# Six of twelve gate projection pairs moved out of the recurrence into a phase of their own, with two thirds of their tokens computed by Strassen's seven products

## The chip, the cores and the metric

The kernel runs on one core of one Trainium2 chip. A core has five engines that run side by side, each through its own instruction stream in order: TensorE for matmuls (PE in the profile, with its weight loads as PEld), VectorE (DVE), ScalarE (ACT), GpSimd (POOL) and SyncE (SP), which here issues every DMA. The metric is the device time of one execution in microseconds (us). Before the change it is 2398.26 us, the median of three runs (2398.25 to 2399.79).

## The reference

One layer of a diffusion backbone is computed for 1024 sample tokens and 128 prompt tokens of width 1024, all in fp32. One wide projection of the modulated input feeds everything:

```python
qm, km, vm, om, gates, qa, ka, va, gm, ga = _split(h @ w_in, SPLITS)
hm, C, n, m = mlstm_bidir(...)                       # recurrence in both directions, 4 heads
hm = rms_norm(hm, ...) * jax.nn.sigmoid(om)
ha = block_attention(...)                            # 8 query heads on 2 key heads
merged = jax.nn.sigmoid(gm) * (hm @ w_bm) + jax.nn.sigmoid(ga) * (ha @ w_ba)
x = layer_norm(ALPHA * x + g1 * (merged @ w_out), ...)
x = layer_norm(ALPHA * x + g2 * (jnp.square(jax.nn.relu(h2 @ w_up)) @ w_down), ...)
```

The change is about `om`, `gm` and `ga`, three gates of 1024 columns each, which nothing needs before the merge that comes after attention.

## The kernel before

**Precision.** Every large fp32 product is made of three matmuls. `split` writes a rounded copy (`hi`, by ACT, line 72) and the remainder (`lo`, by DVE, line 73) of each operand, and `mm3` sums hi·hi, hi·lo and lo·hi in PSUM (lines 78 to 80). So a product over 1024 inputs is 8 blocks of 128 with 3 matmuls each: 24 matmuls.

**Tiling.** The 1152 tokens lie transposed in three blocks `hT[0..2]` of 384 tokens, hi and lo. A *pair* (`proj_pair`) is 256 output columns: it loads its weights (two loads of 512 KB into the two buffers `raw`), splits them, and computes for 3 blocks and 2 halves of 128 columns one tile `g` of 24 matmuls, which DVE copies out of PSUM (line 250) for a store to DRAM. PSUM holds two `g` tiles (`psg`), so the copy of a tile must be done before the tile after next can start. A pair is 144 matmuls of 384 columns. The twelve gate pairs are four each of `om`, `gm`, `ga`, stored in `gad`.

**Stages in order of time.** Start and modulation (to about 143 us); the recurrence `mlstm` over four heads (143 to 969 us); the attention's prologue and attention (to about 1310 us); the gate and output projections; the feed-forward part, whose second half is done by the same Strassen scheme for 768 tokens (`up_halves`, line 1408).

**The recurrence and its filler.** A head is a backward pass of 7 units, each a load of keys and values (`kvt`), a `kv_update` (6 matmuls into `kvp`) and a new state `st` stored to `bsd`; then 9 forward steps of 4 units: scores `sp`, decay `sT` with its split `sh`/`sl`, the output `op` of 18 matmuls, the normalised `hs` that is transposed a step later, and the state update. These are short matmuls with long chains over ACT and DVE between them. PE is kept busy by `filler`, a generator that hands out other matmuls in chunks of 6: key/value projections of the later heads, `q` pairs, the attention's `q`, `k`, `v`, the late half of the modulation (`mod_late`), and at the end all twelve gate pairs. After each unit `pull` takes `left / units` of it, where `left` is the filler's total in the program's own estimate (0.16 us per matmul of 384) less `RESERVE = 26.0`, and `units` is 176 at the start. What is left runs beside the attention's prologue, which loads and splits keys and values (`KH`, `KL`, `VH`, `VL`).

**What sets the order.** Each engine's instructions are put in order when the kernel is built, by a scheduler that works with estimated durations; pieces of code that are written one after the other come out interleaved. On the chip each engine then keeps that order. A tile of a pool that is opened where a closed pool lay waits for the tiles that it overlaps.

## Time and profile before

The profiled execution took 2397.98 us, of which the span from the first to the last instruction is 2396.2 us.

| stage (us from the span's start) | PE busy | DVE busy | DMA busy share |
|---|---|---|---|
| 190 to 340, recurrence, head 0 | 149.85 of 150 | 83.43 | 0.50 |
| 400 to 470, recurrence with attention's q | 66.43 of 70 | 50.44 | 0.48 |
| 640 to 780, recurrence, heads 2 and 3 | 140.00 of 140 | 75.03 | 0.53 |
| 969 to 1010, filler beside the prologue | 41.00 of 41 | 16.17 | 0.43 |
| 1350 to 1400, plain projections | 50.00 of 50 | 15.24 | 0.57 |

PE's busy time is modelled: matmuls overlap in its pipeline, and each row's duration (about 0.33 us for 384 columns) is longer than the distance to the next one. What a matmul costs in a dense stretch is the distance from start to start.

### The profile page before, as it was taken

Reading aid. Unit: us, or ns where it says so; the run is one execution under the profiler, and the core shown is the slowest. Engines: PE = TensorE matmul, PEld = TensorE weight load, DVE = VectorE, ACT = ScalarE, POOL = GpSimd, SP = SyncE. Lnnn points to the kernel's source line nnn. Section 1 sums busy time; section 2 is a strip of 40 time slices with the busy share of each in tenths; the row PEclk is TensorE's granted clock in tenths of the full one; section 3 lists DMA queues with packets and bytes.
Section 4 is the critical chain, followed back from the end, with each engine's and each line's share of the span. In section 5 each row is a group of like instructions: output and inputs, shape, how many; then the busy total and the mean of one; then the engine's idle time right before and its main releaser. Section 6 shows DMA issues by size and latency. Waiting matters only on the chain.

```text
span 2396.2 us, 36004 instructions
## 1 busy us (share of the span) xinstructions
PE 2348.3 (98%) x13294; PEld 2125.0 (89%) x13294; DVE 1494.3 (62%) x2738; ACT 999.6 (42%) x2133; POOL 372.0 (16%) x582
## 2 busy tenths in 40 slices
PE   7999999999999999999999999999999999999997
PEld 4888888788999999989999999889999989999996
DVE  5645645745755564388787345679444686666777
ACT  3323433524433243266666323225333443444444
POOL 1000110201101011144443000010000221111111
PEclk9999999999999999999999999999999999999999
DMA  7265447445654743320001755334443452222223
GB/s 273 90 207 159 128 134 216 138 126 163 196 157 139 216 148 99 118 68 17 17 17 40 228 184 180 121 115 150 140 132 124 152 173 69 64 71 71 71 79 115
DMA packets 229745, 305.71 MB, mean 128 GB/s; under 512 B 18105, under 2 KB 168753, under 8 KB 229569
## 3 DMA queue, kind: packets, MB, share of 16 engines
q1 hardware_dynamic: 229568, 303.41, 40.3%
q8 instruction: 105, 1.72, 0.3%
q14 instruction: 72, 0.58, 0.1%
HBM read 236.55 MB, written 66.79 MB: 127 GB/s over the span
## 4 chain that ended last, share of the span: by engine, by line
PE 87%; DVE 6%; DMA 3%; ACT 2%; issue 1%; POOL 1%; SPq 0%; DVEq 0%; ACTq 0%; POOLq 0%
PE g L78 14%; PE g L80 13%; PE g L79 13%; PE u L1408 4%; PE d L78 3%; PE d L79 3%; PE d L80 3%; PE pp L1408 3%; PE pz L1408 3%; PE t L883 2%; PE u L80 2%; PE u L78 2%; PE u L79 2%; PE pa L79 2%; PE pa L80 2%; PE pa L78 2%
## 5 line engine op out<-in xcount | busy, mean ns | idle before, releaser
L78 PE MATMUL g<-th,wh 128*128 128x384 f32 x1088 | 370.9, 341 | 0.0
L80 PE MATMUL g<-th,wl 128*128 128x384 f32 x1088 | 365.9, 336 | 0.0
L79 PE MATMUL g<-tl,wh 128*128 128x384 f32 x1088 | 364.1, 335 | 0.0
L72 ACT ACTIVATE wh<-raw 128x1024 fp32r<-128x1024 f32 x180 | 188.5, 1057 | 310.8 <-PE d L80 142.0
L73 DVE TENSOR_TENSOR wl<-raw,wh 128x1024 fp32r<-128x1024 f32 x180 | 223.9, 1251 | 127.1 <-ACT wh L72 125.7
L78 PE MATMUL g<-wh,th 128*128 128x512 f32 x600 | 240.6, 401 | 1.4 <-ACT xq L654 0.8
L80 PE MATMUL g<-wh,tl 128*128 128x512 f32 x600 | 236.0, 393 | 0.0
L79 PE MATMUL g<-wl,th 128*128 128x512 f32 x600 | 235.4, 393 | 0.0
L78 PEld LDWEIGHTS g<-th,wh 128*128 128x128 f32 x1088 | 204.4, 188 | 8.6 <-issue 5.9
L80 PEld LDWEIGHTS g<-th,wl 128*128 128x128 f32 x1088 | 204.2, 188 | 0.4 <-issue 0.4
L79 PEld LDWEIGHTS g<-tl,wh 128*128 128x128 f32 x1088 | 204.5, 188 | 0.1
L1199 DVE TENSOR_TENSOR acc<-acc,d 128x512 f32<-128x512 f32 x160 | 109.4, 685 | 58.6 <-PE d L80 56.7
L78 PEld LDWEIGHTS g<-wh,th 128*128 128x128 f32 x600 | 112.8, 188 | 26.7 <-issue 3.8
L80 PEld LDWEIGHTS g<-wh,tl 128*128 128x128 f32 x600 | 112.7, 188 | 23.3
L79 PEld LDWEIGHTS g<-wl,th 128*128 128x128 f32 x600 | 112.9, 188 | 20.7 <-DVE wl L73 1.0
L72 ACT ACTIVATE ph<-t 128x384 fp32r<-128x384 f32 x192 | 91.0, 493 | 70.5 <-PE t L883 70.1
L250 DVE COPY fm<-g 128x384 f32<-128x384 f32 x96 | 53.2, 554 | 98.3 <-PE g L80 96.1
L73 DVE TENSOR_TENSOR pl<-t,ph 128x384 fp32r<-128x384 f32 x192 | 104.7, 548 | 9.0 <-ACT ph L72 7.2
L883 PE MATMUL t<-ident,pe 128*128 128x128 f32 x576 | 96.2, 276 | 6.2 <-DVE pl L73 5.1
L1312 POOL TENSOR_TENSOR wtl<-raw 128x512 f32<-128x512 f32 x16 | 20.7, 1295 | 486.3 <-PE pa L79 252.8
L872 POOL TENSOR_SCALAR pe<-pe,rs 128x1152 f32<-128x1152 f32 x64 | 79.0, 1235 | 55.0 <-DVE rs L871 27.6
L78 PE MATMUL pv<-ph,vh 128*128 128x256 f32 x288 | 85.6, 297 | 1.5 <-DVE tl L73 1.5
(398 smaller groups left out, 5899.9 us busy)
## 6 DMA issues: line engine op xcount, KB each, us to landing
raw<-in_w_up_dram SPq DMA_DIRECT2D x64, 512.0 KB
raw<-in_w_down_dram SPq DMA_DIRECT2D x64, 512.0 KB
raw<-in_w_in_dram SPq DMA_DIRECT2D x44, 512.0 KB
kvt<-kvd SPq DMA_DIRECT2D x64, 257.0 KB
raw<-in_w_mod_dram SPq DMA_DIRECT2D x32, 512.0 KB
kvd<-kvs SPq DMA_DIRECT2D x36, 257.0 KB
uw<-ud SPq DMA_DIRECT2D x72, 128.0 KB
bs<-st SPq DMA_DIRECT2D x32, 258.0 KB
```

The costliest lines, as they stand in the source:

```text
L72: nc.scalar.activation(out=hi, in_=src, func=AF.Copy)
L73: nc.vector.tensor_tensor(out=lo, in0=src, in1=f(hi), op=ALU.subtract)
L78: nc.tensor.matmul(out, lhsT=ah, rhs=bh, start=start and i == 0, stop=False)
L79: nc.tensor.matmul(out, lhsT=ah, rhs=bl, start=False, stop=False)
L80: nc.tensor.matmul(out, lhsT=al, rhs=bh, start=False, stop=stop and i == n - 1)
L250: nc.vector.tensor_copy(out=st[:], in_=g[:, 0:TB])
L872: nc.gpsimd.tensor_scalar(pe[:], pe[:], rs[:, 0:1], 1.0, ALU.mult, ALU.mult)
L883: nc.tensor.transpose(pt[:, k, :], pexp[u][:, kt * 128:kt * 128 + 128], ident[:])
L1199: nc.vector.tensor_tensor(out=y[:, cs], in0=y[:, cs], in1=g[:], op=ALU.add)
L1312: nc.gpsimd.tensor_tensor(out=tmp[i], in0=x, in1=y, op=op)
L1408: nc.tensor.matmul(o, lhsT=x[:, k, :], rhs=y[:, k, :], start=fresh and k == 0 and i == 0, stop=k == 3 and i == 2, skip_group_check=True)
```

## The change

Of the twelve gate pairs five (all `om`, first of `gm`) stay in the recurrence's filler (`NPL = 5`), and the reserve falls from 26 to 12. The filler of the recurrence so has 8 pairs instead of 15. `mod_late` may start a second time within a long job. The last pair (`ga` 3) stays plain and becomes the filler beside the attention's prologue.

The six pairs between them run in a new phase after the recurrence. Their first 384 tokens are computed as before (`plainS`, 48 matmuls, copied out by ACT). The 768 tokens of blocks 1 and 2 are taken as the two halves of a 2x2 block product (columns of the pair, inputs, tokens each halved) by Strassen's scheme in Winograd's form: seven products of 12 matmuls each (line 878 of the changed kernel) instead of eight, 84 matmuls instead of 96. For it

- the four token forms are made once by `t_formsS`: 16 additions (line 796) and 16 subtractions (line 802) on DVE, and 16 splits (ACT and DVE), spread by `building` over the rest of the recurrence's filler;
- per pair, POOL makes four weight combinations (`combS`, line 828 of the changed kernel, 128x512 each), ACT and DVE split them into a ring of three (`ufS`), ACT copies three sums and one result out of PSUM, and DVE makes five sums (line 866);
- new pools `psS` (four PSUM banks) and `sp` take the recurrence's place, and the attention's pools take theirs.

```diff
+    gpairs = [(a + 256 * p, gad[nm][p]) for nm, a in (("om", OM), ("gm", GM), ("ga", GA)) for p in range(4)]
+    NPL, RES = 5, 12.0
...
-        for nm, a in (("om", OM), ("gm", GM), ("ga", GA)):
-            jobs += [(proj_pair(a + 256 * p, gad[nm][p]), 24) for p in range(4)]
+        jobs += [(proj_pair(a, dst), 24) for a, dst in gpairs[:NPL]]
...
-                if c == 8 and mods:
+                if (c == 8 or c == 20 and n == 36) and mods and md is None:
                     md = mods.pop(0)
...
-    left = [6 * FT + 15 * FP - RESERVE]
+    left = [6 * FT + (3 + NPL) * FP - RES]
...
     st1.close()
+    psS = pool(sts_, "psS", 2, space=PSUM)
+    sp_ = pool(sts_, "sp", 1)
+    tS = {nm: tuple(sp_.tile([128, 4, TB], F32R, name="tS" + nm + e) for e in "hl") for nm in ("s1", "s2", "s3", "a22")}
...
+    def t_formsS():
+        src = {"a11": tS["a11"], "b12": tuple(t[:, 0:4, :] for t in hT[2]), "a12": tS["a12"], "s4": tS["s4"]}
+        for k in range(4):
+            full = []
+            for nm, t in src.items():
+                d = sft("f" + nm)
+                nc.vector.tensor_tensor(out=d[:], in0=f(t[0][:, k, :]), in1=f(t[1][:, k, :]), op=ALU.add)
+                full.append(d)
+                yield
+            b11, b12, b21, b22 = full
+            t3 = sft("ft3")
+            for dst, x, y, nm in ((t3, b22, b12, "s3"), (b11, b12, b11, "s1"), (b22, b22, b11, "s2"), (b21, b21, b22, "a22")):
+                nc.vector.tensor_tensor(out=dst[:], in0=x[:], in1=y[:], op=ALU.subtract)
+                split(tS[nm][0][:, k, :], tS[nm][1][:, k, :], dst[:])
+                yield
...
+    def halvesS(slots, c, w, dst, each):
...
+        for j, nm in enumerate(("a11", "a22", "a12", "s2", "s1", "s3", "s4")):
+            b = "xyxpzpz"[j]
+            fresh = b not in bank
...
+            for k in range(4):
+                for i, (x, y) in enumerate(((wh, bh), (wh, bl), (wl, bh))):
+                    nc.tensor.matmul(o, lhsT=x[:, k, :], rhs=y[:, k, :], start=fresh and k == 0 and i == 0,
+                                     stop=k == 3 and i == 2, skip_group_check=True)
...
+    building(fill)
+    preps.append(prepS(spairs[1][0]))
+    for i in range(2):
+        building(plainS(preps[i][1], spairs[i][1]))
+    run(build)
+    for i in range(n):
...
+        halvesS(preps[i][1], comb, fw_, spairs[i][1], each)
+        if "fill" in nxt:
+            fill = nxt["fill"]
+            next(fill)
+        if i + 1 < n:
+            comb, fw_ = nxt["c"], nxt["w"]
+            if i:
+                run(plainS(preps[i + 1][1], spairs[i + 1][1]))
```

How this comes out in the engines' order is shown at three places.

**The filler in the last head, on SP.** Each forward step of the recurrence ends in one store `hmd<-ho`; each `<-fm` is the store of one filler tile of 24 matmuls. Before:

```order
L69 DMA hmd_4_177<-ho 128x256
L66 DMA kvt<-kvd_8_133 128x514
L69 DMA ga_1_245<-fm 128x384
L69 DMA ga_2_246<-fm 128x384
L66 DMA raw<-in_w_in_dram 128x4x256
L69 DMA ga_2_246<-fm 128x384
L66 DMA raw<-in_w_in_dram 128x4x256
L69 DMA hmd_5_178<-ho 128x256
L69 DMA ga_0_247<-fm 128x384 x2
L69 DMA ga_1_248<-fm 128x384
L69 DMA hmd_6_179<-ho 128x256
```

The same place now:

```order
L69 DMA hmd_4_177<-ho 128x256
L66 DMA kvt<-kvd_8_133 128x514
L69 DMA om_1_227<-fm 128x384
L69 DMA om_2_228<-fm 128x384
L69 DMA hmd_5_178<-ho 128x256
L66 DMA raw<-in_w_in_dram 128x4x256
L69 DMA om_2_228<-fm 128x384
L66 DMA raw<-in_w_in_dram 128x4x256
L69 DMA om_0_229<-fm 128x384
L69 DMA hmd_6_179<-ho 128x256
```

Between two step stores there stood three tiles, now two. On PE, in this head, the scores `sp` of a step and its `op` were 36 filler matmuls apart in the usual step, now 24.

**DVE at the end of the recurrence.** `no<-pt` is the recurrence's last small output. Before, what followed were copies of filler tiles (`fm<-g`) and the split of the attention's keys (`kl`):

```order
L646 COPY no<-pt 16x128
L250 COPY fm<-g 128x384 x2
L73 TENSOR_TENSOR kl<-pe,kh 128x512 x2
L250 COPY fm<-g 128x384
L73 TENSOR_TENSOR kl<-pe,kh 128x512 x2
L250 COPY fm<-g 128x384
```

Now the token forms (`Sf...`, `tS...`) stand there. This is the stretch from the second to the third copy, which is repeated twice more:

```order
L250 COPY fm<-g 128x384
L73 TENSOR_TENSOR tSs3l<-Sft_9584,tSs3h 128x384
L73 TENSOR_TENSOR tSs1l<-Sfa_9560,tSs1h 128x384
L802 TENSOR_TENSOR Sfs_9576<-Sfs_9576,Sfa_9560 128x384
L796 TENSOR_TENSOR Sfb_9611<-th,tl 128x384
L802 TENSOR_TENSOR Sfa_9574<-Sfa_9574,Sfs_9576 128x384
L73 TENSOR_TENSOR tSs2l<-Sfs_9576,tSs2h 128x384
L796 TENSOR_TENSOR Sfa_9609<-th,tl 128x384
L73 TENSOR_TENSOR tSa22l<-Sfa_9574,tSa22h 128x384
L796 TENSOR_TENSOR Sfs_9625<-th,tl 128x384
L796 TENSOR_TENSOR Sfa_9623<-th,tl 128x384
L802 TENSOR_TENSOR Sft_9633<-Sfs_9625,Sfb_9611 128x384
```

One more (line 802) follows before the next copy, so 12 DVE instructions stand between one tile's copy and the next, where there were none to two.

**PE in the same stretch.** `g` is a filler tile of the recurrence's last pair, `Sx` the first Strassen product:

```order
L80 MATMUL g<-th,wl 128x384
L878 MATMUL Sx<-th,wh 128x384
L878 MATMUL Sx<-tl,wh 128x384
L878 MATMUL Sx<-th,wl 128x384
L878 MATMUL Sx<-th,wh 128x384
L878 MATMUL Sx<-tl,wh 128x384
L878 MATMUL Sx<-th,wl 128x384
L878 MATMUL Sx<-th,wh 128x384
L878 MATMUL Sx<-tl,wh 128x384
L878 MATMUL Sx<-th,wl 128x384
L878 MATMUL Sx<-th,wh 128x384
L78 MATMUL g<-th,wh 128x384
```

The scheduler has put 10 to 12 matmuls of the first two products between filler tiles, four tiles before the filler ends. From the recurrence's last instruction on PE to the first tile of `plainS` there are 7 whole filler tiles and the rest of one, where 11 whole ones stood before attention's first transposes; beside the attention's prologue there are now 6.

More of the change, by code (lines that the diff above doesn't have):

```diff
@@ L772, in hybrid_step_kernel, with sft @@
     st1.close()
+    sts_ = ctx.enter_context(ExitStack())
+    psS = pool(sts_, "psS", 2, space=PSUM)
+    sp_ = pool(sts_, "sp", 1)
+    tS = {nm: tuple(sp_.tile([128, 4, TB], F32R, name="tS" + nm + e) for e in "hl") for nm in ("s1", "s2", "s3", "a22")}
+    tS["a11"] = tuple(t[:, 0:4, :] for t in hT[1])
+    tS["a12"] = tuple(t[:, 4:8, :] for t in hT[1])
+    tS["s4"] = tuple(t[:, 4:8, :] for t in hT[2])
+    ufS = sp_.tile([128, 6, 512], F32R, name="ufS")
+    cntS = [0]
+    def sft(nm, w=TB):
+        return sp_.tile([128, w], F32, tag=nm, name="S" + nm)
@@ new lines, in hybrid_step_kernel, with prepS @@
+    wiv = kview(w_in)
+    def prepS(a):
+        raws, slots = [], []
+        for q in range(2):
+            raw = rp.tile([128, 1024], F32, tag="raw", name="raw")
+            rv = raw[:].rearrange("p (k n) -> p k n", n=256)
+            load(rv, wiv[:, 4 * q:4 * q + 4, a:a + 256])
+            hi = wp.tile([128, 1024], F32R, tag="wh", name="wh")
+            lo = wp.tile([128, 1024], F32R, tag="wl", name="wl")
+            split(hi[:], lo[:], raw[:])
+            raws.append(rv)
+            slots.append(tuple(t[:].rearrange("p (k n) -> p k n", n=256) for t in (hi, lo)))
+        return raws, slots
@@ new lines, in combS @@
+    def combS(raws):
+        a11, a21 = raws[0][:, :, 0:128], raws[0][:, :, 128:256]
+        a12, a22 = raws[1][:, :, 0:128], raws[1][:, :, 128:256]
+        c = {}
+        for nm, x, y, op in (("s1", a21, a22, ALU.add), ("s2", "s1", a11, ALU.subtract), ("s3", a11, a21, ALU.subtract),
+                             ("s4", a12, "s2", ALU.subtract)):
+            t = sft("c" + nm, 512)[:].rearrange("p (k n) -> p k n", n=128)
+            nc.gpsimd.tensor_tensor(out=t, in0=c[x] if isinstance(x, str) else x, in1=c[y] if isinstance(y, str) else y, op=op)
+            c[nm] = t
+        return c
@@ new lines, in plainS, with formS @@
+    def plainS(slots, dst):
+        for m in range(2):
+            g = gtile()
+            w = [tuple(t[:, k % 4, 128 * m:128 * m + 128] for t in slots[k // 4]) for k in range(KT)]
+            yield from mm3g(g[:, 0:TB], [(w[k], (hT[0][0][:, k, :], hT[0][1][:, k, :])) for k in range(KT)], 2, C384)
+            st = fmp.tile([128, TB], F32, tag="fm", name="fm")
+            nc.scalar.activation(out=st[:], in_=g[:, 0:TB], func=AF.Copy)
+            store(dst[0][:, m, :], st[:])
+    def formS(src):
+        j = cntS[0] % 3
+        cntS[0] += 1
+        hi, lo = (ufS[:, j + 3 * e, :].rearrange("p (k n) -> p k n", n=128) for e in range(2))
+        split(hi, lo, src)
+        return hi, lo
@@ new lines, in hybrid_step_kernel, with building, each @@
+    spairs = gpairs[NPL:11]
+    n = len(spairs)
+    preps = [prepS(spairs[0][0])]
+    comb = combS(preps[0][0])
+    fw_ = begin_forms(comb)
+    build = t_formsS()
+    def building(gen):
+        for _ in gen:
+            next(build, None)
+            next(build, None)
+    building(fill)
[4 more added lines that the diff above has]
+    for i in range(n):
+        nxt = {}
+        def each(j):
+            if j == 3:
+                if i + 1 < n:
+                    nxt["c"] = combS(preps[i + 1][0])
+            elif j == 5 and i + 2 < n:
+                preps.append(prepS(spairs[i + 2][0]))
+            elif j == 5 and i + 2 == n:
+                nxt["fill"] = proj_pair(*gpairs[11])
+            elif j == 6 and i + 1 < n:
+                nxt["w"] = begin_forms(nxt["c"])
+        halvesS(preps[i][1], comb, fw_, spairs[i][1], each)
+        if "fill" in nxt:
+            fill = nxt["fill"]
+            next(fill)
+        if i + 1 < n:
+            comb, fw_ = nxt["c"], nxt["w"]
+            if i:
+                run(plainS(preps[i + 1][1], spairs[i + 1][1]))
@@ L775, in hybrid_step_kernel @@
+    sts_.close()
     st2 = ctx.enter_context(ExitStack())
```

38 lines of the change are left out of this document (added).

## The prediction

> **What bounds the kernel now.** First the page: the busy line and the chain of work that ended last.
>
> ```profile
> span 2396.2 us, 36004 instructions
> ...
> PE 2348.3 (98%) x13294; PEld 2125.0 (89%) x13294; DVE 1494.3 (62%) x2738; ACT 999.6 (42%) x2133; POOL 372.0 (16%) x582
> ...
> PE 87%; DVE 6%; DMA 3%; ACT 2%; issue 1%; POOL 1%; SPq 0%; DVEq 0%; ACTq 0%; POOLq 0%
> ```
>
> TensorE is busy 98% of the span and holds 87% of the last chain. Busy time alone can hide slow matmuls, so the next view is by stages; columns are the stretch, its length, then busy time of PE, PEld, DVE, ACT and POOL with counts, PE clock, DMA share, GB/s.
>
> ```profile
> 143.00:190.00 47.00, 46.46 (x241) 37.08 (x240) 24.96 (x60) 12.82 (x32) 3.42 (x19) 1.00 0.71 214
> 190.00:340.00 150.00, 149.85 (x828) 125.01 (x827) 83.43 (x190) 61.78 (x171) 21.43 (x53) 1.00 0.50 148
> 340.00:400.00 60.00, 60.00 (x342) 54.21 (x341) 32.58 (x72) 19.96 (x49) 4.06 (x15) 1.00 0.65 200
> 400.00:470.00 70.00, 66.43 (x355) 53.56 (x354) 50.44 (x99) 39.00 (x123) 16.84 (x29) 1.00 0.48 144
> 540.00:640.00 100.00, 99.36 (x571) 86.60 (x570) 66.46 (x141) 48.38 (x153) 19.72 (x33) 1.00 0.56 171
> 780.00:836.00 56.00, 56.00 (x351) 52.97 (x350) 29.39 (x67) 15.96 (x38) 3.64 (x9) 1.00 0.73 224
> 836.00:969.00 133.00, 132.24 (x844) 128.51 (x843) 72.87 (x158) 51.77 (x119) 16.70 (x26) 1.00 0.40 122
> 1010.00:1060.00 50.00, 47.30 (x320) 43.58 (x318) 34.54 (x77) 28.69 (x76) 20.67 (x28) 1.00 0.23 73
> ```
>
> The clock is full throughout. In these stretches of the recurrence PE idles 0.54 + 0.15 + 3.57 + 0.64 + 0.76 = 5.7 us, most of it in 400 to 470, where the attention's q is prepared beside it. So the kernel is bound by the number of matmuls, and whatever the filler covers is really covered.
>
> **The term that gains: 12 matmuls less per pair.** What a plain matmul costs is read from start to start in a stretch that has nothing else (timeline, the first and the last of 217 starts, nine tiles of 24 between), what a Strassen product costs from one run of seven products in the feed-forward part (stages, line 1408 alone).
>
> ```profile
> 1360.12 0.33 PE L78 MATMUL g<-th,wh 128*128 128x384 f32 x1
> ...
> 1397.56 0.33 PE L78 MATMUL g<-th,wh 128*128 128x384 f32 x1
> ...
> 1928.20:1942.93 14.73, 14.72 (x84) 14.54 (x83) 1.00 0.60 190
> ```
>
> Plain: 37.44 / 216 = 0.1733 us. The two later blocks of a pair are 96 of them, 16.64 us. The 84 of the seven products take 14.72 us, 0.1752 each. Six pairs gain 6 x 1.92 = **11.5 us**. The 48 matmuls per pair on the first block, the seven other pairs, the recurrence itself and all weight loads stay in number.
>
> **The token forms: DVE against the filler's copies.** PE's filler tiles need their PSUM bank copied by DVE, and 12 form instructions stand between two copies. Durations and spacing are those of the same work in the feed-forward part (timeline), the copy's and the split's from the page.
>
> ```profile
> 1656.23 0.55 DVE L1131 TENSOR_TENSOR va<-th,tl 128x384 f32<-128x384 f32 x1
> 1656.69 0.55 DVE L1131 TENSOR_TENSOR vs<-th,tl 128x384 f32<-128x384 f32 x1
> ...
> L73 DVE TENSOR_TENSOR wl<-raw,wh 128x1024 fp32r<-128x1024 f32 x180 | 223.9, 1251 | 127.1 <-ACT wh L72 125.7
> L250 DVE COPY fm<-g 128x384 f32<-128x384 f32 x96 | 53.2, 554 | 98.3 <-PE g L80 96.1
> ```
>
> One starts 0.47 us after the other, though each lasts 0.55. So 13 instructions from copy to copy take 6.1 us. PE has in that time a tile, 24 x 0.1733 = 4.16 us, and 10 to 12 Strassen matmuls, 1.8 to 2.1 us: 5.9 to 6.3 us. The two are even. Ahead of it DVE has two weight splits, three weight forms and six token instructions, about 7.5 us, while PE has two free banks, 8.3 us. I charge 0.2 us for each of the three stretches and 0.6 us for POOL's combinations, which run in the middle: **1.2 us**. From both sides: nothing, or, if each instruction took its whole 0.55 us, 48 x 0.08 = 3.9 us more.
>
> POOL slows DVE where both read; the feed-forward part shows how much (groups, 1920 to 2200 us, the same split beside POOL and away from it; below them POOL's own combination on the page).
>
> ```profile
> L73 DVE TENSOR_TENSOR uf<-wtl,uf 128x512 fp32r<-128x512 f32 x18 | 21.1, 1174 | 11.2 <-ACT uf L72 11.2
> ...
> L73 DVE TENSOR_TENSOR uf<-wth,uf 128x512 fp32r<-128x512 f32 x18 | 12.4, 689 | 12.9 <-ACT uf L72 12.8
> ...
> L1312 POOL TENSOR_TENSOR wtl<-raw 128x512 f32<-128x512 f32 x16 | 20.7, 1295 | 486.3 <-PE pa L79 252.8
> ```
>
> The split that meets POOL takes 0.49 us longer. Three combinations, those of the second pair, fall among the forms: 1.5 us of DVE, of which 0.6 us reaches PE through a bank. The Trainium skill, "SBUF — State Buffer", "Who interferes with whom", says that a DVE instruction with two SBUF inputs and a POOL instruction that reads SBUF exclude each other for the whole instruction. By that rule DVE would lose up to 3 x 1.3 = 3.9 us there; this trace shows less than half of it per meeting.
>
> **The recurrence with less cover.** By the program's numbers the filler per unit falls from 596 / 176 = 3.39 us to 449 / 176 = 2.55 us. What hangs on it is the slack of each chain (timeline, last head: scores, decay, its split, the product; the earlier step's normalised output and its transpose; then a backward unit).
>
> ```profile
> 877.24 0.35 DVE L621 TENSOR_SCALAR hs<-hs,ss 128x256 f32<-128x256 f32 x1 [0.77 <-POOL ss L620]
> 879.93 0.61 PE L578 MATMUL sp<-qt,kT 128*128 128x128 f32 x4
> 881.56 0.55 DVE L73 TENSOR_TENSOR sl<-sT,sh 128x256 fp32r<-128x256 f32 x1 [0.55 <-ACT sh L72]
> 883.50 0.38 PE L562 MATMUL pt<-ident,hs 128*128 128x128 f32 x2
> 887.13 0.28 PE L78 MATMUL op<-vh,sh 128*128 128x258 f32 x1
> ...
> 801.11 0.42 DVE L73 TENSOR_TENSOR wkl<-wk,wkh 128x256 fp32r<-128x256 f32 x1
> 803.58 0.28 PE L78 MATMUL kvp<-vh,wkh 128*128 128x258 f32 x1
> ```
>
> `sl` ends at 882.11, 5.0 us before its product; with 12 matmuls less (2.1 us) 2.9 us stay. `hs` ends 5.9 us before its transpose; 18 matmuls less in that place, 3.1 us, leave 2.8. `wkl` has 2.05 us, and its unit loses about 1. So the usual step still waits for nothing. The waits that are there already grow: cover falls by a quarter, and I let the 5.7 us of idle time grow by half, **2.8 us**, the bounds being 0 and 12 us (0.07 us in each of 176 units).
>
> **Attention starts with less cover.** The keys' loads and splits follow the phase's last stores on SP, and 6 tiles (25 us) beside them are ample, since the prologue waits only for its DMAs. But the first units no longer have three tiles behind their scores. Their chain is these (groups of attention, then the page):
>
> ```profile
> L865 DVE TENSOR_REDUCE nm<-sa 128x1 f32<-128x768 f32 x52 | 49.5, 951 | 5.4 <-PE sa L80 5.4
> ...
> L868 ACT ACTIVATE pe<-sa,nm 128x768 f32<-128x768 f32 x52 | 46.5, 895 | 0.0
> L867 ACT ACTIVATE pe<-sb,nm 128x384 f32<-128x384 f32 x52 | 30.2, 581 | 26.3 <-DVE nm L866 21.6 <-PE t L883 2.9 <-DVE tl L73 0.4
> ...
> L872 POOL TENSOR_SCALAR pe<-pe,rs 128x1152 f32<-128x1152 f32 x64 | 79.0, 1235 | 55.0 <-DVE rs L871 27.6
> ```
>
> 0.95 + 0.58 + 0.90 + 1.24 and some 1.2 us of small steps are 4.9 us, against 18 matmuls, 3.1 us, of the next two units: **1.5 us**, bounds 0 and 4.9.
>
> **Inside the phase** a pair takes 14.7 + 8.3 = 23 us on PE and some 8 us each on DVE and ACT, and POOL 4 x 1.3 us; the loads are two per pair as before, but wait for POOL to be done with `raw`. The place without plain tiles, between the first two pairs, is the tightest. **0.4 us**, bounds 0 and 3.
>
> **Sum.** -11.5 + 1.2 + 2.8 + 1.5 + 0.4 = -5.6 us against the profiled execution's 2397.98 us (0.3 us under the median of the runs): **2392.4 us**. 0.2%, 4.8 us, is about what a measurement of this kernel can tell from no change.
>
> **Rivals.**
> *The cover's loss takes most of the gain.* If the idle time of 400 to 470, where DVE is busy 72% already, and that of the later q stretch (540 to 640) double, 4.2 us, and each head's backward pass loses 0.5 us more, the recurrence costs 6.2 us instead of 2.8: 2395.8 us, no change. For it: 3.57 of 5.7 us idle time lie there. Against: the slacks above.
> *POOL and DVE exclude each other.* Each of three combinations stops DVE for its whole 1.3 us, 3.9 us that reach PE through the banks in full: 3.3 us over what I charge, 2395.7 us, no change. For it: DVE and PE are even there, so no slack takes it up. Against: 0.49 us per meeting. This is the rule of the Trainium skill named above; by it this rival holds.
> *The recurrence becomes bound by DMA; slower.* Its bytes stay, but its time shrinks by about a quarter. From the stages: 143 to 190 holds 0.71 x 47 = 33 us of full DMA and will have about 34; 780 to 836 holds 41 and will have 43; 340 to 400 holds 39 for 46. As long as the queues can be kept over nine tenths full, nothing is lost. If only 0.8 can be used, the three need 42, 51 and 49 us, 19 us more if all of it reached PE; I count 11, since loads that run ahead take some of it up: 2403.4 us. It makes the kernel slower from a usable share of about 0.8 downwards. Against it stand two short stretches in which DMA ran full while PE was never idle:
>
> ```profile
> 135.00:140.00 5.00, 5.00 (x26) 3.55 (x25) 1.25 (x6) 0.00 (x0) 0.00 (x0) 1.00 0.96 284
> 160.00:165.00 5.00, 4.99 (x26) 3.91 (x24) 1.67 (x4) 1.42 (x4) 0.57 (x1) 1.00 1.01 264
> ```
>
> *The change doesn't do what it says.* If a product waited for its accumulating bank (ACT must copy `Sx` before the third product adds to it), 0.15 us in each of the 42 products would be 6.3 us and the gain gone: 2398.7 us. The feed-forward part does the same at 0.1752 us per matmul, so hardly.
>
> **How the numbers follow.** My forecast has 0.46; the cover's loss 0.27, the exclusion 0.07, no gain in the products 0.04, together 0.38 for no change; DMA 0.16 for slower. The range reaches down to 2385.5, the whole gain at no cost and 1 us of today's idle time gone with it, and up to 2402.5: costs of 16 us, two thirds of the sum of their upper bounds (5.1 + 12 + 4.9 + 3), which takes in part of the DMA case.
>
> **What would show it.** In the changed profile: 84 matmuls of line 878 in 14.7 us; PE idle under 2 us between the last `hs` transpose and the first tile of `plainS`; under 9 us of idle time in the recurrence, which should end near 812 us (969 less 147 us of filler by the program's numbers, each of 0.16 us being 0.1733); DMA shares under 0.95 in its backward passes; attention's first transposes within 2 us of the scores of its third unit. Waits of PE for `wkl` or `sl`, or single gaps over 2 us among the forms, would make the prediction wrong.

## The result, and the profile after

The changed kernel takes **2420.71 us** (median of four runs, 2418.94 to 2422.81) beside 2399.03 us for the kernel before on the same chip: ratio 1.0087, 95% interval 1.0075 to 1.0100. It is 21.7 us slower; 2392.4 was forecast, and the range ended at 2402.5. The profiled execution took 2418.94 us, 20.96 more than the one of before.

The page first: span, busy line, and shares of the chain that ended last.

```profile
span 2417.1 us, 36076 instructions
...
PE 2346.6 (97%) x13222; PEld 2115.2 (88%) x13222; DVE 1534.5 (63%) x2804; ACT 1037.3 (43%) x2209; POOL 408.1 (17%) x606
...
PE 55%; DVE 4%; ACT 2%; issue 1%; DMA 1%; POOL 1%; DVEq 0%; ACTq 0%; POOLq 0%
```

The 72 matmuls are gone (13294 to 13222), and PE is still busy 97%. Where the time went is read by stages. The view by stretches of the changed kernel: first the recurrence from its first `kvp` to its last `hs` transpose, then the first part of the phase, its rest, and attention. Columns as in the prediction: stretch, length, busy PE, PEld, DVE, ACT, POOL, then clock, DMA share, GB/s.

```profile
145.00:830.00 685.00, 664.92 (x3900) 571.31 (x3900) 428.82 (x968) 306.16 (x839) 105.50 (x234) 1.00 0.57 171
830.00:872.00 42.00, 37.34 (x205) 36.59 (x204) 36.91 (x60) 13.09 (x24) 14.89 (x7) 0.96 0.20 61
872.00:1021.00 149.00, 146.62 (x845) 145.98 (x844) 50.77 (x70) 43.42 (x72) 29.46 (x23) 1.00 0.33 103
1021.00:1332.00 311.00, 300.83 (x2132) 278.00 (x2132) 243.63 (x572) 202.47 (x516) 129.25 (x193) 1.00 0.10 30
```

The same stretches of the kernel before (recurrence, then the prologue's filler, then attention):

```profile
143.00:969.00 826.00, 820.33 (x4823) 730.97 (x4821) 468.73 (x1021) 323.62 (x854) 108.11 (x234) 1.00 0.53 159
969.00:1001.00 32.00, 32.00 (x187) 31.84 (x186) 11.73 (x18) 6.49 (x11) 4.15 (x6) 1.00 0.50 155
1001.00:1310.00 309.00, 299.86 (x2141) 279.99 (x2140) 239.74 (x567) 198.70 (x511) 129.69 (x192) 1.00 0.09 27
```

Length less busy PE is PE's idle time: the recurrence went from 5.67 to **20.08 us**, the phase from 0.00 to 4.66 + 2.38 = 7.04, attention from 9.14 to 10.17. That is 22.5 us more, but -11.5 + 22.5 is only half of the 21 us by which the profiled execution is longer. The rest is in the busy column: a row is longer than the distance to the next one, so a matmul that starts a little late leaves no idle time. A second measure catches it: the distance from each matmul's start to the next, less the usual step of its shape (0.1733 us for 384 columns, 0.227 for 512, 0.104 to 0.120 for the short ones), summed and called *lost time* below. It went from 39.8 to 58.9 us in the recurrence, 0.1 to 8.9 in the phase, 27.0 to 30.7 in attention and 33.2 to 34.0 elsewhere: 32.4 us more. With 72 matmuls fewer (12.5 us by the same steps) that makes 19.9, and 20.96 was measured; the short matmuls' steps are rough, so a sum of this kind holds to about 1 us.

Who is waited for in the recurrence, changed kernel (columns: in all us, times, longest):

```profile
PE pt L550 <- ACT ho L565: 3.9, 4, 1.3
PE g L79 <- DVE wl L73: 3.7, 4, 1.5
PE pt L562 <- ACT qs L685: 2.3, 2, 1.4
PE g L78 <- ACT xq L654: 1.9, 1, 1.9
PE kvp L78 <- ACT wkh L72: 1.4, 3, 1.0
```

The same list of the kernel before begins so:

```profile
PE pt L550 <- ACT ho L565: 1.6, 3, 0.8
PE pt L683 <- ACT kT L552: 1.6, 1, 1.6
PE g L78 <- ACT xq L654: 0.8, 1, 0.8
```

No single wait took over. Many grew, and ACT stands behind most: `ho`, `qs` and `kT` are its copies out of the one PSUM bank `t`, which all transposes share, and `xq` its copy out of a `g` bank.

The idle time can be split in two ways. The first is by the recurrence's own passes. The four backward passes idle 0.5 us before and 7.9 us after, the forward passes 5.1 and 12.2 us. So half of the rise lies in the backward passes, which are a fifth of the recurrence's time. The last one, in the kernel before and after:

```profile
792.50:828.60 36.10, 36.10 (x227) 34.27 (x226) 19.47 (x45) 8.64 (x20) 0.79 (x2) 1.00 0.72 221
```

```profile
682.80:719.40 36.60, 33.98 (x208) 30.30 (x208) 25.45 (x53) 15.55 (x41) 5.71 (x6) 1.00 0.80 243
```

The DMA share of these passes is 0.80 to 0.89 after the change (0.58 to 0.86 before). After the change PE waits there mostly for the unit's own chain (`wkh`, `wkl`, `st`) and for the weights' splits (`wl`).

The second split is by the filler's jobs, whose stretches take in the backward passes. There the lost time lies in the six token jobs (keys/values, attention's k/v and q): 21.8 us before, 44.1 after (some 8 us of the rise are only the matmuls of six more modulation halves that now run in them, about 1.4 us each, for which the steps above have no price; in the pair jobs they are missing). One of them, attention's second `q` job, in the kernel before and after:

```profile
558.50:623.30 64.80, 64.16 (x343) 53.13 (x342) 43.73 (x95) 34.48 (x119) 15.06 (x26) 1.00 0.52 154
```

```profile
609.10:687.60 78.50, 73.20 (x405) 57.53 (x404) 52.75 (x113) 43.74 (x144) 20.18 (x34) 1.00 0.46 139
```

The stretch of the same job now has 405 matmuls, the job's own among them, instead of 343, since more units of the recurrence and a second modulation half fall on it, and with them 144 instead of 119 ACT instructions. Its idle time goes from 0.64 to 5.30 us.

### The profile page after: what moved, and what is told of

The parts are those of the page before. It is cut to its first block, busy times and chain, and to the rows that moved or that the text cites. A ratio compares the mean times of both kernels' runs of the same rounds, so it can differ in the third digit from the quotient of the medians.

```text
span 2417.1 us, 36076 instructions
## 1 busy us (share of the span) xinstructions
PE 2346.6 (97%) x13222; PEld 2115.2 (88%) x13222; DVE 1534.5 (63%) x2804; ACT 1037.3 (43%) x2209; POOL 408.1 (17%) x606
## 4 chain that ended last, share of the span: by engine, by line
PE 55%; DVE 4%; ACT 2%; issue 1%; DMA 1%; POOL 1%; DVEq 0%; ACTq 0%; POOLq 0%
PE g L79 5%; PE g L78 5%; PE g L80 5%; PE u L1575 4%; PE d L78 3%; PE d L80 3%; PE d L79 3%; PE pp L1575 3%; PE pz L1575 2%; PE t L1050 2%; PE u L80 2%; PE u L78 2%; PE u L79 2%; PE pa L79 2%; PE pa L80 2%; PE pa L78 2%
## 5 line engine op out<-in xcount | busy, mean ns | idle before, releaser
L78 PE MATMUL g<-th,wh 128*128 128x384 f32 x896 | 304.9, 340 | 4.7 <-DVE fm L250 4.7
L80 PE MATMUL g<-th,wl 128*128 128x384 f32 x896 | 301.6, 337 | 0.0
L79 PE MATMUL g<-tl,wh 128*128 128x384 f32 x896 | 300.2, 335 | 0.0
L78 PEld LDWEIGHTS g<-th,wh 128*128 128x128 f32 x896 | 168.8, 188 | 9.9 <-DVE fm L250 5.5
L79 PEld LDWEIGHTS g<-tl,wh 128*128 128x128 f32 x896 | 169.0, 189 | 0.0
L80 PEld LDWEIGHTS g<-th,wl 128*128 128x128 f32 x896 | 168.6, 188 | 0.0
L78 PE MATMUL u<-th,wh 128*128 128x384 f32 x256 | 85.7, 335 | 0.0
```

The lines of the kernel that those rows point to most:

```text
L78: nc.tensor.matmul(out, lhsT=ah, rhs=bh, start=start and i == 0, stop=False)
L79: nc.tensor.matmul(out, lhsT=ah, rhs=bl, start=False, stop=False)
L80: nc.tensor.matmul(out, lhsT=al, rhs=bh, start=False, stop=stop and i == n - 1)
```

## The experiments

Times are medians of device runs; each was compared with the kernel before on the same chip (2398.6 to 2400.4 us in these comparisons). Where a run is set against the changed kernel's 2420.71 us, the two can come from different chips, whose times of the kernel before lie up to 1.8 us apart.

### Is it Strassen, or the cover?

**The six pairs done plainly in the phase's place.**

```diff
-        jobs += [(proj_pair(a, dst), 24) for a, dst in gpairs[:NPL]]
+        jobs += [(proj_pair(a, dst), 24) for a, dst in gpairs]
...
-    sts_ = ctx.enter_context(ExitStack())
...
-    sts_.close()
+    pull(left[0] + 6 * FP)
```

> The changed kernel with its six pairs computed plainly, as 96 + 48 matmuls each, in the place of the phase: no Strassen product, no token form, no combination, one pair left for the prologue as in the changed kernel. Everything ahead of the last hs transpose is the changed kernel's. Theory thin cover (the loss is made in the recurrence, whose filler was taken away): the waits of the recurrence stay at the changed kernel's level (PE idle about 20 us between 143 and 830 us) though nothing of Strassen is there; 2416 to 2422 us, no better than the changed kernel, since it lacks the 11.5 us gain but also the phase's own waits. Rival: the phase (token forms, combinations, drained filler) makes the loss: then this kernel is back at the kernel before plus at most 5 us, 2399 to 2404 us.

2419.47 us, ratio 1.0089 (1.0071 to 1.0107). Its recurrence and the stretch behind it, by stretches:

```profile
144.00:830.00 686.00, 664.26 (x3897) 570.85 (x3896) 428.70 (x968) 306.17 (x838) 105.31 (x234) 1.00 0.57 171
830.00:1012.00 182.00, 182.00 (x1052) 181.60 (x1051) 47.03 (x67) 21.02 (x25) 1.45 (x4) 1.00 0.33 103
```

21.74 us idle in the recurrence and nothing behind it. So the whole 20 us of slowdown is there without a single Strassen product, and the phase, with its 11.5 us gain, gives nothing back: by lost time it pays 8.7 us in the phase and 4.2 in attention (30.7 against 26.5; this kernel also keeps about 10 us more filler for the time after the first scores).

**Three Strassen pairs instead of six.**

```diff
-    NPL, RES = 5, 12.0
+    NPL, RES = 8, 12.0
```

> The changed kernel with eight instead of five plain pairs left in the recurrence, so three Strassen pairs. Three pairs' gain is lost (3 x 1.92 = 5.8 us). Theory thin cover: the recurrence gets 75 us of filler back and its idle time falls from about 20 us to about 10; sum about -4 us, 2413 to 2419 us. Rival, the loss is fixed in the phase: 2420.7 + 5.8 = 2426 us.

2422.37 us, ratio 1.0101 (1.0083 to 1.0119): a miss for thin cover. The recurrence idles 17.4 us instead of 20.1, though 75 us of filler came back. The backward passes recovered (lost time 18 to 8 us), the forward passes did not. Part of that is the clock: in this trace two waits of PE in the forward passes, 2.0 and 3.7 us long, each came with 3.4 us at a granted clock of 0.50 (from 431 and from 670 us), which the changed kernel's recurrence doesn't have. The rest was still unknown.

### Is it the modulation's new order?

**Only the new condition, in the kernel before.**

```diff
-                if c == 8 and mods:
+                if (c == 8 or c == 20 and n == 36) and mods and md is None:
```

> The kernel before with one edit alone: the condition of the filler that starts a modulation half, as the changed kernel has it (a second half in each 36-tile job, so that they end nine jobs earlier). All pairs stay plain and the recurrence keeps its whole filler. The runs so far left open whether the recurrence waits because it has less cover or because the modulation halves (two DMAs of 512 KB through the two raw buffers, a transpose-like product in the t bank) now meet the token jobs: with three pairs given back its backward passes came down from 18 us of lost time to 8, as before, but its forward passes stayed at 47 us (32 before). Theory modulation: the forward passes rise by 8 to 15 us, 2407 to 2414 us. Theory thin cover: within 3 us of 2399.3.

2405.12 us, ratio 1.0021 (1.0010 to 1.0031): 5 us, between the theories. The recurrence idles 11.1 us.

**The old condition, with eight pairs.** The edit is the reverse of the last.

> The changed kernel with eight plain pairs in the recurrence and the old condition for the modulation halves, one per job (17 jobs are enough for 16 halves). Against the run with eight pairs and the new condition, 2422.4 us. Theory modulation: 8 to 15 us less, 2407 to 2414 us. Theory thin cover: within 3 us of 2422.4.

2427.95 us, ratio 1.0112 (1.0095 to 1.0129): no gain, but 5.6 us more.

**One half per job in the nine first jobs, two in each later pair.**

```diff
-                if (c == 8 or c == 20 and n == 36) and mods and md is None:
+                if c in ((8,) if i < 9 else (2, 12)) and mods:
...
-                if c >= 8 and c % 2 and md is not None:
+                if c >= 2 and c % 2 and md is not None:
```

> The changed kernel with the modulation halves placed otherwise: one per job in the first nine jobs, as before, and two in each of the next pair jobs, so that no token job has two. Theory modulation: the token jobs' lost time falls from 44 us by 5 to 8 us, 2412 to 2416 us. Theory density alone: within 3 us of 2420.7, as the eight-pair run with the old condition showed no gain.

2425.59 us, ratio 1.0112 (1.0096 to 1.0127), 4.9 us more. The new order costs 5 us in the kernel before, but taking it back, in full or in part, gains nothing once the cover is thin. It doesn't explain the loss.

### Is it DMA?

**The gate rows loaded once per head.**

```diff
-            uw = mt([128, 2, 2, 128], "uw", 2)
-            for i in range(2):
-                load(uw[:, i, :, :], ud[i, :, h, s * 128:s * 128 + 128].partition_broadcast(128))
+            if s == 0:
...
+            uw = qts["uw"]
```

> The changed kernel with the two broadcast loads of the gate rows (uw, 2 x 128 KB) issued only at the first tile of each head; the other eight tiles of a head compute with the first tile's rows, so the numbers of the recurrence are left wrong while every other instruction stays. 64 of 72 such DMAs, 8.4 MB of about 100 MB in the recurrence, are gone. Theory DMA-bound (the queue is full in the shortened recurrence and weight splits and states come late): the waits for wl, wkl and kT fall, and the time by 8 to 15 us, to 2406 to 2413 us. Theory thin cover with compute chains as the limit: within 3 us of 2420.7.

2422.6 us, ratio 1.0097 (1.0082 to 1.0112), 21.1 us idle.

**The keys and values loaded once per backward pass.**

```diff
+            kv, v = load_kv(h, s, None if s == 7 else kv)
```

> The changed kernel with one load of the keys and values (kvt, 257 KB) per backward pass instead of seven; the other six units compute with the first tile's rows, so the backward states are left wrong while all other instructions stay. 1.5 MB less of some 9.5 MB in each backward pass. Theory DMA: the backward passes' lost time falls from 18 to 8 to 11 us, 2411 to 2414 us. Rival, their waits are for the weights' splits and the chain of wk on ACT and DVE: within 3 us of 2420.7.

2418.03 us, ratio 1.0082 (1.0067 to 1.0097); the backward passes' lost time fell from 18.1 to 16.0 us. The DMAs that these two runs leave out are worth 0 and some 2 us of the 20. No run leaves out the weights' loads (`raw`), so for the backward passes, where the DMA share is highest, it stays open how much of the rise is DMA.

### Which chains did the cover hide?

**`hs` transposed into the scores' bank.**

```diff
-            pt = ttile([128, 2, 128])
+            pt = ps1.tile([128, 2, 128], F32, tag="s", bufs=1, name="pt")
```

> The changed kernel with one line altered: the transposes of a step's normalised output (hs) write the bank of the scores (tag s) instead of the single bank t that they share with the transposes of kvt, xq and the modulation. Theory: in the recurrence PE waits above all for that one bank to be emptied by ACT (the waits pt<-ident,kvt for ACT ho alone are 3.9 us in the changed kernel): these waits vanish and the time falls by 4 to 8 us, to 2413 to 2417 us. Rival, the bank is only where a general lateness of ACT, DVE and DMA shows first: the waits come out at other tiles and the time stays within 2 us of 2420.7.

2417.04 us, ratio 1.0076 (1.0061 to 1.0091): 3.7 us less, and 16.6 us idle. The interval of this ratio overlaps the changed kernel's, as do those of the next one and of the copies' run below; the idle time says more. In the last head's forward steps the lost time falls from 5.4 to 1.5 us.

**The mask added on DVE.** The place that led to it, timeline of the changed kernel:

```profile
732.97 1.21 DVE L73 TENSOR_TENSOR wl<-raw,wh 128x1024 fp32r<-128x1024 f32 x1
...
733.13 1.99 POOL L554 TENSOR_TENSOR pm<-uw,mask 128x256 f32<-128x256 f32 x1 [2.74 <-DVE sT L580]
...
733.95 0.38 PE L562 MATMUL pt<-ident,hs 128*128 128x128 f32 x2
...
735.15 0.69 ACT L556 ACTIVATE pm<-pm,tmA 128x128 f32<-128x128 f32 x2 [1.59 <-POOL pm L554]
...
735.75 0.60 ACT L565 ACTIVATE ho<-pt,mgn 128x128 f32<-128x128 f32 x2
...
736.40 0.44 PE L550 MATMUL pt<-ident,kvt 128*128 128x128 f32 x2 [1.21 <-ACT ho L565]
```

POOL's addition starts 0.16 us after DVE's split and takes 1.99 us; most of the 36 take about 0.74 us. ACT's exponential waits for it, ACT's `ho`, whose transpose was done by 734.3, stands behind that in ACT's queue, the bank is not emptied, and PE stops 1.21 us.

```diff
-            nc.gpsimd.tensor_tensor(out=pm[:], in0=uw[:, 0, :, :], in1=mask[:], op=ALU.add)
+            nc.vector.tensor_tensor(out=pm[:], in0=uw[:, 0, :, :], in1=mask[:], op=ALU.add)
```

> The changed kernel with the addition of the mask to the gate rows (pm<-uw,mask) on DVE instead of POOL. In two places of the changed trace this addition took 1.99 us beside a weight split of DVE, ACT's exponential waited for it, and the output copies of ACT behind that held the t bank (PE waits of 1.3 us). Theory POOL and DVE exclude each other in the recurrence and that is what became late: the waits pt<-ident,kvt go (3.9 us) and others of ACT with them: 4 to 8 us less, 2413 to 2417 us. Rival, DVE is the late engine: each of 36 additions puts 0.35 us more on it, and the time rises by 0 to 6 us.

2416.38 us, ratio 1.0066 (1.0051 to 1.0081), 15.5 us idle: 4.3 us less.

**Without ACT's four squares per token tile.**

```diff
-        for i in range(nh):
-            nc.scalar.activation(out=jk[:], in_=xq[:, i, :], func=AF.Square, accum_out=ss[:, i:i + 1])
+        nc.vector.memset(ss[:, 0:nh], 1.0)
```

> The changed kernel without the four squares with sums on ACT in the preparation of each tile of attention's q and k (replaced by a memset of the sums, so these vectors are left unnormalised): 90 ACT instructions less in the token jobs of heads 0 to 2. Theory, ACT's queue is what the shortened cover shows first there (xq, qs and ho stand in one queue, and the t bank waits for them): the waits pt<-ident,xq and pt<-ident,hs, some 6 us, go: 2413 to 2417 us. Rival, the queue of ACT is only one of several and the waits move to DVE and the weights: within 3 us of 2420.7.

2408.54 us, ratio 1.0034 (1.0022 to 1.0046): **12.2 us less**, more than expected. The control is the same edit in the kernel before:

> The control: the kernel before without the four squares with sums on ACT per tile of attention's q and k (a memset in their place, so these vectors stay unnormalised), the edit that took 12 us off the changed kernel. Theory: ACT's queue became the late one because the cover went; before it was covered, and at most 4 of the 5 to 6 us of idle time of the recurrence are there to win: 2395 to 2400 us. Rival, the squares cost any recurrence about 12 us: 2386 to 2389 us.

2396.47 us, ratio 0.9987 (0.9978 to 0.9996): **2.1 us**. The two recurrences by stretches, of the changed kernel and of the one before, each without the squares:

```profile
143.00:819.00 676.00, 662.78 (x3900) 572.58 (x3898) 427.64 (x994) 278.30 (x660) 107.56 (x230) 1.00 0.58 173
```

```profile
146.00:971.00 825.00, 819.22 (x4821) 731.58 (x4821) 469.97 (x1045) 293.26 (x673) 110.13 (x230) 1.00 0.53 159
```

28 us less of ACT's work takes idle time from 20.1 to 13.2 us where the cover is thin. Where it is whole the row has 5.8 us, as without the edit (5.7), though the profiled execution was the slowest of its kernel, 4.0 us over the median; the times decide here. The gain over the control is 12.2 - 2.1 = 10.1 us, about half of the slowdown. It lies in the forward passes, whose idle time falls from 12.2 to 6.5 us (5.1 in the kernel before); the backward passes keep 6.7 of their 7.9.

So about half of what the cover hid is the cost of the squares in the token jobs. In which way they cost it is not shown. They fill ACT's queue, but they are also a link of the job's own chain (`xq`, squares, POOL's factor, `xq` again), and the edit takes out both. That ACT is busy only 45% of the recurrence (306 of 685 us) says nothing against the queue, since ACT's instructions run in order. One place, timeline of the changed kernel:

```profile
633.27 1.10 POOL L554 TENSOR_TENSOR pm<-uw,mask 128x256 f32<-128x256 f32 x1 [3.35 <-DVE sT L580]
...
634.41 0.69 ACT L556 ACTIVATE pm<-pm,tmA 128x128 f32<-128x128 f32 x2 [0.76 <-POOL pm L554]
...
635.01 0.57 ACT L654 ACTIVATE xq<-g 128x512 f32<-128x512 f32 x1
...
635.64 0.50 PE L78 MATMUL g<-wh,th 128*128 128x512 f32 x1 [1.89 <-ACT xq L654]
```

What held `xq` here was not a square but the step's mask: ACT idled 0.76 us for POOL's `pm`, and `xq` stood behind its exponentials.

**The control for the bank and the mask**, both edits in the kernel before:

> The control: the kernel before with the first two of those edits (hs into the scores' bank, the mask on DVE). Theory thin cover: with its cover whole, these chains have slack, at most 1.6 us of waits for the t bank are there to win: 2397 to 2400 us. Rival, the edits speed up any recurrence: 6 to 8 us less, 2391 to 2393 us.

2399.67 us, ratio 1.0000 (0.9990 to 1.0009): nothing. Those chains have slack there.

### Cover put back, or spread otherwise

**TensorE's cover alone**, by repeated matmuls:

```diff
+                for _ in range(rep):
+                    mm3(g[:, 0:TB], terms[0:2])
+                    yield C384 * 6
...
+    left = [6 * FT + (3 + NPL) * 1.75 * FP - RES]
```

> The changed kernel with cover of TensorE alone put back: in each of the eight pairs that the recurrence still has as filler, the first six matmuls of a tile are done four times instead of once (a new start each time, so the result stays), 864 matmuls or 149.7 us more at 0.1733 us, and the filler's budget raised by the same. No DMA, copy, split or modulation is added, and the order of the modulation halves stays new. Theory thin cover: the idle time of the recurrence goes back, 12 to 19 us of it, so 2420.7 + 149.7 - 12 to 19 = 2551 to 2558 us. Rival, the waits come from what is beside (the modulation halves' new places, the density of DMA, ACT or DVE work of the jobs): nothing goes back, 2568 to 2573 us.

2565.48 us, ratio 1.0687 (1.0669 to 1.0705): 5 us came back of 12 to 19, a miss. Its token jobs lost 40.2 us, about as in the kernel before with the new modulation order (37.8), so much of what did not come back may be that order's; another 6 us stand in one pair job, which lost 8.4 us where the same job of that kernel lost 2.6: one wait of 3.19 us for `ho`, and from 731.4 us on 6.8 us at a clock of 0.50. These matmuls also come in blocks of 18 at the start of a tile, so cover in this form is not the cover of whole pairs.

**More filler beside the token jobs, less beside the pairs.**

```diff
-            pull(left[0] / max(units, 1))
+            pull(3.39 if big[0] else 1.83 if len(done) < 9 else left[0] / max(units, 1))
```

> e_mods2 with the same amount of filler spread unevenly: while a token job runs, 3.39 us of filler per unit (the rate of the kernel before), beside the pair jobs of the first nine 1.83, and what is left evenly over the rest. Theory density (a token job costs when more recurrence units run beside it; a pair needs no cover of its own): the token jobs' lost time goes back to 22 to 28 us, the pairs lose up to 5 us: 2402 to 2409 us. Rival, cover as such: what the token jobs win the thin pairs lose, 2412 to 2421 us.

2440.08 us, ratio 1.0164 (1.0147 to 1.0182): 14.5 us more than its even twin with the same modulation order. The recurrence idles 31.7 us (22.5 in the twin), and the pairs pay: by idle time the token jobs go from 17.4 to 12.8 us, the pairs from 5.1 to 18.9. One of the late pair jobs, beside the last head, by stretches:

```profile
749.70:806.00 56.30, 50.42 (x333) 43.64 (x332) 38.06 (x96) 25.48 (x63) 6.29 (x12) 1.00 0.70 219
```

5.9 us idle in one job, where an evenly covered one in the changed kernel idles 1.3:

```profile
727.50:765.80 38.30, 37.03 (x241) 35.97 (x240) 24.32 (x56) 17.65 (x45) 6.09 (x9) 1.00 0.49 146
```

So the pairs need their cover too, and of these two spreads the even one is the better.

### The phase, and the best that could be joined

**The last filler tiles copied by ACT beside the token forms.** The place, timeline of the changed kernel:

```profile
840.79 0.34 PE L80 MATMUL g<-th,wl 128*128 128x384 f32 x1
...
841.66 0.55 DVE L796 TENSOR_TENSOR Sfs<-th,tl 128x384 f32<-128x384 f32 x1
842.13 1.22 DVE L73 TENSOR_TENSOR wl<-raw,wh 128x1024 fp32r<-128x1024 f32 x1
843.26 0.55 DVE L802 TENSOR_TENSOR Sft<-Sfs,Sfb 128x384 f32<-128x384 f32 x1
843.73 0.55 DVE L802 TENSOR_TENSOR Sfa<-Sfb,Sfa 128x384 f32<-128x384 f32 x1
...
844.20 0.55 DVE L250 COPY fm<-g 128x384 f32<-128x384 f32 x1
...
844.80 0.44 PE L78 MATMUL g<-th,wh 128*128 128x384 f32 x1 [3.67 <-DVE fm L250]
```

The tile was done at 841.1 us, its copy started at 844.20, behind a weight split and three form instructions in DVE's order.

```diff
+                if acp:
+                    nc.scalar.activation(out=st[:], in_=g[:, 0:TB], func=AF.Copy)
```

> The changed kernel with the copies of the last plain tiles beside the token forms (fm<-g of the filler drained in the phase) on ACT instead of DVE. Theory: between 830 and 872 us DVE (88% busy) is the bound, PE waits up to 3.8 us for a copy that queues behind form instructions, and the clock falls to 0.96 after it; on ACT (31% busy) the copies come at once: the phase's lost time falls from 8.9 to 3 to 5 us, the time to 2415 to 2418 us. Rival, the forms themselves are late (the first products wait for Su, 2.1 us): the wait moves from the copies to the first product, within 2 us of 2420.7.

2415.28 us, ratio 1.0065 (1.0049 to 1.0082): 5.4 us less. The stretch of the forms in this kernel:

```profile
830.00:872.00 42.00, 39.92 (x228) 39.24 (x228) 34.28 (x54) 18.19 (x34) 14.05 (x7) 1.00 0.26 80
```

2.08 us idle instead of 4.66, and the clock is full (0.96 before).

**These three joined** (bank, mask, copies):

> The changed kernel with three edits that each helped alone: hs transposed into the bank of the scores (3.7 us less), the mask added on DVE (4.3 us less), the filler's last copies on ACT (5.4 us less). The first two both took away the 2.8 us of t-bank waits in the last head, so they don't add in full: 2409 to 2412 us. Still slower than the kernel before, if the rest of the recurrence's loss is cover as such.

2409.93 us, ratio 1.0038 (1.0023 to 1.0053), 14.3 us idle in the recurrence.

**The three joined with the uneven spread:**

> e_uneven together with the three edits of the combined run (hs into the scores' bank, the mask on DVE, the filler's last copies on ACT). If density and those edits add, 10 us under the combined run's 2409.9: 2396 to 2402 us, about the kernel before. If the loss is cover as such, 2406 to 2411 us.

2427.54 us, ratio 1.0121 (1.0105 to 1.0136): the spread undoes it.

**The three, and the squares on POOL with a sum on DVE:**

```diff
+        nc.gpsimd.tensor_tensor(out=jk[:, 0:nh, :], in0=xq, in1=xq, op=ALU.mult)
+        nc.vector.tensor_reduce(ss[:, 0:nh], jk[:, 0:nh, :], AX.X, ALU.add)
```

> The combined run's three edits, and in place of the four ACT squares per tile one multiplication on POOL (all four heads of the tile) and one sum on DVE; the result stays the reference's. Theory: most of the 12 us that the squares cost under thin cover come back, less what POOL and DVE now take: 2400 to 2404 us, the kernel before within 0.2%. Rival, POOL's multiplication is in the same chain and is longer than the four squares: 2408 to 2412 us.

2418.45 us, ratio 1.0081 (1.0067 to 1.0095): 8.5 us more than without. ACT is relieved (274 us busy in the recurrence instead of 303 in the joined run), and yet PE's waits for ACT's `xq` are the longest of this kernel, 4.1 us. So fewer instructions in ACT's queue alone don't bring the time back. The job's chain is longer now; POOL's product alone takes 1.38 us (groups of POOL in this kernel, 400 to 520 us), but that it is what became late is not shown:

```profile
L663 POOL TENSOR_TENSOR qjk<-xq 128x512 f32<-128x512 f32 x9 | 12.4, 1383 | 27.5 <-ACT xq L659 27.5
```

No version with the six pairs taken out of the recurrence came under the kernel before.

## Why the prediction was wrong, point by point

**12 matmuls less per pair, -11.5 us: right.** Line 878 alone, by stretches, in the last pair of the phase:

```profile
994.29:1008.86 14.57, 14.57 (x84) 14.41 (x84) 1.00 0.08 28
```

84 matmuls in 14.57 us, 14.72 forecast. The second pair (16.8 us) and the third (15.3) still met late operands.

**The recurrence with less cover, 2.8 us with bounds 0 and 12: this step failed.** It came to 14.4 us by idle time and 19.1 by lost time. The step read the slack of three chains (`sl` 2.9 us, `hs` 2.8, `wkl` about 1) in the last head and in one backward pass, and let that stand for "the usual step". Beside pairs, in the forward steps of the last head, it does nearly hold; the changed kernel's row has 2.6 us idle:

```profile
719.40:829.90 110.50, 107.92 (x699) 105.28 (x698) 65.09 (x151) 48.73 (x120) 15.60 (x27) 1.00 0.42 129
```

But all three readings came from places where the filler was pairs. In the token jobs ACT and DVE have the job's work besides, and there the chains run through ACT's queue and the `t` bank; no row of such a place was used for the slack. In the backward passes the reading fails beside pairs too: in the very pass that it was taken from, PE now waits 1.0 us for `st` and 0.8 for `wkl`, which was to keep 1 us, and the four passes idle 7.4 us more. Then the size: half of 5.7 us, and a bound of 0.07 us for each of 176 units, have no mechanism behind them. That the step is the one that failed is shown by the plain pairs, which lose the same 20 us with the same recurrence. The removal of the squares (12.2 us under thin cover, 2.1 under full) shows where about half of it lies.

**The rivals.** "The cover's loss takes most of the gain" had the right mechanism and named the right place, the stretches of attention's q; doubling their idle time was too little, and so was 0.5 us for each backward pass, where it came to 1.9. "The recurrence becomes bound by DMA" had the right sign; the two runs that took DMAs away gained nothing and 2.7 us, which speaks against it as the main cause, and the weights' loads were not tried. That POOL and DVE exclude each other was put in the phase, and it shows there, changed kernel:

```profile
845.71 7.37 POOL L828 TENSOR_TENSOR Scs<-raw 128x512 f32<-128x512 f32 x2 [6.73 <-DMA raw<-in_w_in_dram]
...
851.86 1.64 DVE L73 TENSOR_TENSOR tSs1l<-Sfa,tSs1h 128x384 fp32r<-128x384 f32 x1
...
859.79 0.44 PE L78 MATMUL g<-th,wh 128*128 128x384 f32 x1 [0.99 <-DVE fm L250]
```

POOL's first combination here takes 5.8 us, beside ten DVE instructions with two SBUF inputs one after the other; one that meets none takes 1.3. Then three DVE instructions beside the three combinations took 1.18, 1.64 and 1.64 us instead of 0.55, 2.8 us more, and PE waited 0.99 us for the next copy behind them. So the price for DVE, 2.8 us, was nearer to the rival's 3.9 us than to the 1.5 us of the prediction, and about 1 us of it reached PE. The 0.49 us per meeting, which the prediction held against this rival, is a mean: in the kernel before the split takes 0.69 us alone and, when a combination is already running, 0.69 us and all but 0.14 us of what the combination still has to run (1.07 us with 0.52 left, 1.27 with 0.72 left). That is a full exclusion that DVE met late, and it doesn't speak against the rival. In the recurrence, too, taking POOL's instruction away gave 4.3 us.

**The token forms, 1.2 us (0 to 5.1), and inside the phase, 0.4 us (0 to 3): too small, within their bounds by idle time.** They cost 4.66 and 2.38 us. The forms' step set durations against PE's time and found them even; it did not ask in which order DVE takes them. PE's waits from 828 to 1110 us, changed kernel:

```profile
PE g L78 <- DVE fm L250: 4.7, 2, 3.7
...
PE Sp L878 <- DVE Su L866: 1.9, 1, 1.9
```

One copy behind other work stopped PE 3.7 us. In the phase the one place is the second pair, which follows the first without plain tiles between, as named: `Sp` waits 1.9 us for `Su`.

**Attention, 1.5 us (0 to 4.9): 1.0 by idle time, 3.7 by lost time,** within the bounds. (The step's own figures, 4.9 less 3.1, give 1.8.)

**What stays open.** One by one the squares, the mask and the bank gave 12.2, 4.3 and 3.7 us; the mask and the bank don't add in full (with the copies 10.8 us together, 13.4 one by one), and leaving the squares out was not joined with them. Whether the squares act through ACT's queue or through the job's chain is open, and so is what share of the backward passes' 7.4 us is DMA. The modulation's order shifts the time by 5 us either way, by how its pieces fall beside the units. Why cover by repeated matmuls brought only 5 us back is not settled beyond what is said there.

## What to carry to other kernels

Filler that keeps TensorE busy is not spare time: taking 923 matmuls, some 160 us, of it out of this recurrence cost 20 us, and that cost is a charge on any faster way to do the same work elsewhere. Read the slack of the chains in the stretch where the helpers' queues are fullest, not in the quietest one, and take an engine's place in order, not its busy share, as what can be late. Before the faster method is built, move the plain work to its place and time that: one run would have shown the 20 us.

## What the runs showed of the hardware

The gap of 3.67 us cost more than itself. Two stretches around its end, changed kernel:

```profile
842.00:846.30 4.30, 1.50 (x9) 1.50 (x9) 4.30 (x9) 1.11 (x3) 0.59 (x1) 1.00 0.69 164
846.30:849.70 3.40, 3.40 (x12) 3.40 (x12) 3.40 (x8) 0.93 (x2) 3.40 (x1) 0.50 0.49 168
```

From 1.5 us after work had resumed the granted clock was 0.50 for 3.4 us, and some ten matmuls of 384 columns started 0.320 us apart instead of 0.173, 1.5 us more. After the wait of 1.9 us for `Su` the spacing was 0.173 to 0.185 us from the second matmul on. The Trainium skill, "TensorE: Matmul & The Clock Gate", Part 1, says that a free-running window of about 3.4 us without work halves the clock. These two gaps agree with that; other traces here don't. The same wait of attention is 1.88 us long in the changed kernel and in the run with `hs` in the scores' bank. In the first the clock stays full:

```profile
1038.86 0.44 PE L78 MATMUL sb<-kh,qhi 128*128 128x384 f32 x1 [1.88 <-ACT pe L1034]
...
1039.00:1042.30 3.30, 2.96 (x14) 2.05 (x15) 2.03 (x6) 2.25 (x6) 2.26 (x4) 1.00 0.14 40
```

In the second it is halved:

```profile
1037.56 0.44 PE L78 MATMUL sb<-kh,qhi 128*128 128x384 f32 x1 [1.88 <-ACT pe L1034]
...
1038.00:1041.30 3.30, 3.30 (x12) 2.93 (x11) 1.30 (x5) 1.94 (x6) 1.98 (x3) 0.50 0.12 25
```

In the copies' run three gaps of about 0.5 us within 3 us were followed by a clock of 0.50 as well (from 483.4 us). So here a gap well under 3.4 us could halve the clock, and the same gap could leave it alone; what decides is not shown. Such stretches are part of what some runs lose: the profiled recurrences of the kernel before, the changed kernel and the plain pairs have none, the changed kernel with eight plain pairs and the kernel before with the new modulation order two each, the uneven spread five. By the 1.5 us above that is an estimate of 3 and of 7 to 8 us.
